# Two heads at a time on the array's halves, columns spread by transposes, and the modulation's products moved to TensorE

## The chip, the cores and the metric

The kernel runs on one core of one Trainium2 chip. The metric is the device time of one execution in microseconds. Times are shown as the median of several runs, with the lowest and the highest; a profile is of one execution, and its span is the time from its first to its last instruction.

## The reference

The program is a stack of four residual blocks on 256 positions of width 1024, in fp32. The first block has two layers; each layer mixes four branches (retention, short convolution, conformer convolution, windowed attention) on the sequence `x` and, in layer 0, on a context of 256 positions too. A second block of a recurrence, a gated linear attention and two feed-forward networks follows. The change touches the modulation of the first block, its attention, and the normalizations all over.

```python
def ada_modulation(cvec, w, b):
    m = jax.nn.silu(cvec) @ w + b                 # 1024 -> 3072
    return jnp.split(m, 3, axis=-1)

# per layer l of the first block, for c (sequence) and c_ctx (context)
shift_x, scale_x, gate_x = ada_modulation(c, w_mod[l], b_mod[l])
shift_c, scale_c, gate_c = ada_modulation(c_ctx, w_mod[l], b_mod[l])
hx = modulate(rmsnorm(x, norm_w[l]), shift_x[:, None], scale_x[:, None])
...
x = x + gate_x[:, None] * out_x

def windowed_gqa(q, k, v, k_ctx, v_ctx, sink):    # 8 heads of 64, 2 kv heads, window 128
    s_loc = jnp.einsum('bnqhgd,bnkhd->bnhgqk', qb, kw) * scale   # masked
    s_ctx = jnp.einsum('bnqhgd,bchd->bnhgqc', qb, k_ctx) * scale
    p = jax.nn.softmax(jnp.concatenate([s_loc, s_ctx, s_sink], axis=-1), axis=-1)
    o = (jnp.einsum('bnhgqk,bnkhd->bnqhgd', p_loc, vw)
         + jnp.einsum('bnhgqc,bchd->bnqhgd', p_ctx, v_ctx))
```

In layer 0 the context's own 256 queries attend to the context's keys as well.

## The kernel before

Activations lie transposed, channels on partitions and positions along the free dimension: tiles of 128 channels by 256 positions, or by 512 in layer 0 (sequence and context side by side). Every projection is a sum of three fp32r products: `load` fetches a weight chunk of 128x1024 (512 KB), ScalarE rounds it to `wh`, VectorE makes the rest `wl`, and `mm3` multiplies high by high, high by low and low by high. Chunks come in a fixed order (`mixer_chunks`); four are held at a time, and `drop` lets the next be fetched.

Beside this stream, work is queued. `hiq` holds generators (attention, convolutions, layer norm, retention), each `yield` with a cost; `loq` holds (cost, function) pairs for the rest. After each output tile `pump(us)` adds credit and runs the queues: `hiq` at full rate, `loq` at `ratio` times the rate (0.5 in layer 0 until the layer norm is done, then 1.4), from the eleventh pump of layer 0 on, with a credit of at most 4. A scheduler then orders each engine's instructions by this emission order and its own estimate of when each is ready; each engine works strictly through its list.

The modulation of layer 0's first two thirds (shift and scale) is made at the start by `products` and `columns`: eight matmuls whose stationary operand has 32 columns (two are used: the silu of `c` and of `c_ctx`), in four column strips of the array, then a copy to SBUF and two small matmuls with the selector `sel` that add the four strips and turn rows into columns. The rest (layer 0's gate and all of layer 1, 32 tiles of 128 columns) is queued on `loq` by `queue_mods`: `fetch_row` brings 128x1024 of the transposed weight, and `matvec` runs one VectorE pass per condition with an accumulator (line 487). Behind them in `loq` stand 96 such rows, with one pass each, for the modulation of the second block (`adaT`); `flush_lo` runs what is left at the end of a layer. The rows' pool has two buffers, and the SyncE queue that fetches rows fetches the weight chunks too.

`att_head` handles one head: scores for each block of 128 queries (64 contraction rows, on partitions 0 to 63 or 64 to 127 by the head's parity), a VectorE reduction that scales, masks and takes the maximum (lines 1077 and 1089), exponentials on ScalarE, a division on VectorE, transposes of the probabilities on TensorE (line 1110), and products with the values (64 stationary columns) into the head's half of a PSUM tile that two heads share (`outs`). `attention` runs the eight heads in a pipe of two.

`spread` makes a 128x128 tile whose rows all repeat one column: an fp32 product of the broadcast column with the identity. Normalizations use it, two to eight at a time.

PSUM has four banks for projections (`psm`) and four for all else (`psa`).

Of the kernel before, what the change touches and what calls it, by code (L numbers as in the profile page):

```python
# [18 lines left out]
P = 128  # L19
D = 1024  # L20
KT = 8
# [83 lines left out]
class Core:  # L105
# [324 lines left out]
    def spread(self, out, col):  # L430

        self.mmul(out, col.to_broadcast([P, P]), self.ident)
# [26 lines left out]
    def silu_load(self, name):  # L459
        t = self.adp.tile([P, 1024], F32, tag="sb", bufs=2, name="sb_" + name)  # L460
# [30 lines left out]
    def queue_mods(self, sc, sx):  # L491
        A, cst = self.A, self.cst
        self.done_mods = [0, 0, 0]
        self.gate = [cst.tile([P, 8, 2], F32, name=f"gate{l}") for l in range(2)]

        def one(l, t):
            m = self.mod[l]
            self.matvec([sc, sx], [m[:, t, 0:1], m[:, t, 1:2]])

        def fin(l):  # L500
            m = self.mod[l]
            lo = 16 if l == 0 else 0
            self.tt(m[:, lo:24, :], m[:, lo:24, :],
                    self.par("b_mod", l * 24 + lo, 24 - lo).unsqueeze(2).to_broadcast([P, 24 - lo, 2]), ALU.add)
            self.ts(self.gate[l], m[:, 16:24, :], 0.5, ALU.mult)
            if l == 1:
                self.stt(self.acol, m[:, 8:16, :], 1.0,
                         self.par("norm_w", 8, 8).unsqueeze(2).to_broadcast([P, KT, 2]), ALU.add, ALU.mult)
            self.done_mods[l] = 1
# [42 lines left out]
    def start(self):  # L552
# [26 lines left out]
        s32 = self.T(S).rearrange("p (k n) -> p k n", k=KT)  # L579
# [5 lines left out]
        def products(g):  # L585

            ps = self.psa()[:, :S]
            for kk in range(KT):
                c = slice((kk % 2) * S, (kk % 2 + 1) * S)
                o = 32 * (kk % 4)  # L590
                nc.tensor.matmul(out=ps[o:o + 32, :], lhsT=s32[:, kk, :], rhs=raws[g][kk // 2][:, c],
                                 start=kk < 4, stop=kk > 3, skip_group_check=True)
            rws[g] = self.rowp.tile([P, 512], F32, tag="row", name=self.nm("row"))[:, :S]
            self.act(rws[g], ps)
# [17 lines left out]
        sel = cst.tile([P, 2], F32, name="sel")  # L612
        nc.vector.tensor_reduce(out=sel, in_=self.ident.rearrange("p (u m) -> p m u", u=4)[:, 0:2, :], axis=AX.X, op=ALU.add)
        def columns(g):
            pm = self.psa()[:, 0:4]
            for t in range(2):
                self.mmul(pm[:, 2 * t:2 * t + 2], rws[g][:, t * P:(t + 1) * P], sel)
            k = 2 * (g // 2)
            p3 = pm.rearrange("p (t n) -> p t n", n=2)
# [104 lines left out]
    def prepare(self):  # L724
        cst = self.cst
        with self.behind():
# [7 lines left out]
            self.queue_mods(*[self.silu2_rows(self.silu_load(n)) for n in ("c", "c_ctx")])  # L734
# [131 lines left out]
    def mixer(self, l, hs, N, first, mod, norm):  # L866
# [193 lines left out]
        outs = {}  # L1060

        def att_head(h):
            t, u = divmod(h, 2)
            g = h // 4
            r = slice(64 * u, 64 * u + 64)
            sink = self.par("att_sink", l * 8 + h)
            nr = 2 * NS
            mx, sm, es = self.small(nr), self.small(nr), self.small(nr)
            ss = []
            for i in range(2):  # L1070
                ps = self.psa()
                lq = qs[t][r, i * P:(i + 1) * P]
                c0 = 0 if i == 0 else S
                self.mmul(ps[:, c0:c0 + S], lq, kd[g][r, 0:S])
                self.mmul(ps[:, S - c0:2 * S - c0], lq, kd[g][r, S:2 * S])
                s = self.T()
                nc.vector.tensor_tensor_reduce(out=s, in0=ps, in1=msk[i], scale=0.125, scalar=sink,
                                               op0=ALU.add, op1=ALU.max, accum_out=mx[:, i:i + 1])
                ss.append(s)
                yield 0.7  # L1080
            if NS == 2:
                ps = self.psa()
                s = self.T()
                for i in range(2):
                    c = slice(i * S, (i + 1) * S)
                    self.mmul(ps[:, c], qs[t][r, S + i * P:S + (i + 1) * P], kd[g][r, S:2 * S])
                for i in range(2):
                    c = slice(i * S, (i + 1) * S)
                    nc.vector.tensor_tensor_reduce(out=s[:, c], in0=ps[:, c], in1=msk[0][:, S:], scale=0.125,
                                                   scalar=sink, op0=ALU.add, op1=ALU.max,  # L1090
                                                   accum_out=mx[:, 2 + i:3 + i])
                    ss.append(s[:, c])
                yield 0.8
            self.ts(mx, mx, -1.0, ALU.mult)
            self.act(es, mx, AF.Exp, bias=sink)
            for i, s in enumerate(ss):
                self.act(s, s, AF.Exp, bias=mx[:, i:i + 1], accum_out=sm[:, i:i + 1])
            yield 0.1
            self.tt(sm, sm, es, ALU.add)
            nc.vector.reciprocal(out=sm, in_=sm)  # L1100
            for i, s in enumerate(ss):
                self.ts(s, s, sm[:, i:i + 1], ALU.mult)
            yield 0.2 + 0.6 * NS
            PT = []
            for i in range(1 + NS):
                pt, p = self.psa(), self.T()
                src = ss[i] if i < 2 else None
                for kk in range(4):
                    blk = ss[i][:, kk * P:(kk + 1) * P] if i < 2 else ss[2 + kk // 2][:, (kk % 2) * P:(kk % 2 + 1) * P]
                    nc.tensor.transpose(pt[:, kk * P:(kk + 1) * P], blk, self.ident)  # L1110
                self.act(p, pt)
                PT.append(p)
                yield 0.1
            if u == 0:
                outs[t] = self.psa()
            po = outs[t]
            for i in range(nr):
                toks = ((0, 1, 2, 3), (2, 3, 0, 1), (2, 3), (2, 3))[i]
                src = PT[i] if i < 2 else PT[2][:, (i - 2) * S:(i - 1) * S]
                for kk, tk in enumerate(toks):  # L1120
                    self.mmul(po[r, i * P:(i + 1) * P], vt[:, tk * P + g * 64:tk * P + g * 64 + 64],
                              src[:, kk * P:(kk + 1) * P], kk == 0, kk == len(toks) - 1)
                if i == 1:
                    yield 0.1
            if u == 1:
                self.act(qs[t], po[:, :N])
                if t == 3:
                    st["att"] = 1
# [692 lines left out]
def build(nc, tc, A):  # L1821
    with ExitStack() as ctx:
        k = Core(nc, tc, ctx, A)
        with ExitStack() as c1:
            k.adp = c1.enter_context(tc.tile_pool(name="adp", bufs=2, reuse_waits="tile"))
            k.setup()
            k.t2 = c1.enter_context(tc.tile_pool(name="t2", bufs=58, reuse_waits="tile"))
# [7 lines left out]
def pack(a):  # L1835
# [10 lines left out]
    wmT = wm.transpose(0, 2, 1).reshape(48, P, 1024)  # L1846
# [9 lines left out]
        "c": f("c").reshape(1, 1024), "c_ctx": f("c_ctx").reshape(1, 1024), "c_2": f("c_2").reshape(1, 1024),  # L1856
        "wmodN": wm[0][:, 0:2048].reshape(4, 2, P, 2, 4, 256)[:, :, :, ::-1].transpose(4, 3, 0, 2, 1, 5).reshape(8, 4, P, 512),
        "wmodT": wmT[16:48],
# [27 lines left out]
```

## Time and profile before

| | |
|---|---|
| median of 3 runs | 1828.62 us (1828.25 to 1831.88) |
| the profiled execution | 1827.48 us, of which its span is 1825.4 us |
| TensorE (PE) busy | 1772.5 us, 97% |
| VectorE (DVE) busy | 1395.3 us, 76% |
| ScalarE (ACT) busy | 892.6 us, 49% |
| read from HBM | 298.61 MB, 164 GB/s over the span |

A busy share is the time in which at least one instruction of the engine was at work, so overlapping matmuls count once. The duration of a matmul record reaches from its start to its modelled end; in a stream the records start closer together than they last. PE is the matmuls, PEld the loads of the stationary operand, POOL is GpSimd, SP is SyncE. `pm` are tiles in the projections' banks, `pa` tiles in the others, `wr` raw weight chunks, `ad` the modulation's rows, `t`, `r` and `s` working tiles, `junk` the unused product of a matrix-vector pass. PEclk is the granted TensorE clock as a share of 2.4 GHz.

### The profile page before, as it was taken

What the parts mean: (1) busy time and instruction counts of PE and PEld (TensorE: products, weight loads), DVE (VectorE), ACT (ScalarE), POOL (GpSimd) and SP (SyncE); (2) the same over time, 40 slices, a digit from 0 to 9 for tenths busy, and PEclk for the clock granted to TensorE, in tenths of its full rate; (3) what the DMA queues carried; (4) which work ended last, traced back from release to release, by engine and by line L of the source; (5) the groups of instructions that cost most, each with busy time, mean ns of one, the idle gap of its engine ahead of it and who ended that gap; (6) DMA issues with size and microseconds to landing.
All of it is one profiled execution on the core that took longest, in us unless ns stands there. A gap on an engine that the chain in (4) does not pass through costs nothing.

```text
span 1825.4 us, 29814 instructions
## 1 busy us (share of the span) xinstructions
PE 1772.5 (97%) x11604; PEld 1589.0 (87%) x11604; DVE 1395.3 (76%) x2564; ACT 892.6 (49%) x1517; POOL 9.4 (1%) x33
## 2 busy tenths in 40 slices
PE   8999999899999998999999999999999999999998
PEld 5788888688978777798999989988999999989998
DVE  4897689975687888899559666778888679788774
ACT  5424432422342223455453455677676656657663
POOL 0000000000000000000000000000000000000000
PEclk9999999999999999999999999999999999999999
DMA  8443234344557787744345335553455643345553
GB/s 335 136 138 105 71 104 159 130 162 163 176 187 263 266 267 264 249 147 132 116 131 171 109 115 175 187 183 104 152 195 179 180 139 105 116 132 193 185 172 117
DMA packets 94300, 301.59 MB, mean 165 GB/s; under 512 B 10048, under 2 KB 11840, under 8 KB 94160
## 3 DMA queue, kind: packets, MB, share of 16 engines
q1 hardware_dynamic: 90528, 292.11, 48.3%
q0 software_dynamic: 1152, 4.19, 0.6%
q10 hardware_dynamic: 2480, 3.39, 0.6%
q8 instruction: 91, 1.49, 0.3%
q14 instruction: 49, 0.40, 0.1%
HBM read 298.61 MB, written 1.05 MB: 164 GB/s over the span
## 4 chain that ended last, share of the span: by engine, by line
PE 79%; DVE 9%; DMA 6%; ACT 3%; issue 3%; SPq 0%; DVEq 0%; ACTq 0%
PE pm L189 60%; PE pa L189 17%; DMA ad<-adaT 5%; DVE junk L487 2%; DVE wl L169 2%; ACT t L166 2%; DVE t L186 1%; PE pa L1110 1%; DVE t L169 1%; ACT wh L166 1%; DMA t<-wmodN 1%; PE pa L539 1%; PE pa L1703 1%; PE pa L400 1%; DVE x L169 0%
## 5 line engine op out<-in xcount | busy, mean ns | idle before, releaser
L189 PE MATMUL pm<-r,wh 128*128 128x256 f32 (+2 forms) x5344 | 1217.3, 322 | 30.5 <-ACT r L166 18.1
L189 PEld LDWEIGHTS pm<-r,wh 128*128 128x128 f32 x5344 | 891.6, 191 | 124.3 <-ACT r L166 25.1
L189 PE MATMUL pm<-r,wl 128*128 128x256 f32 (+2 forms) x2672 | 848.1, 319 | 0.5 <-DVE wl L169 0.5
L166 ACT ACTIVATE wh<-wr 128x1024 fp32r<-128x1024 f32 (+1 forms) x408 | 426.1, 1049 | 558.1 <-PE pm L189 385.7
L169 DVE TENSOR_TENSOR wl<-wr,wh 128x1024 fp32r<-128x1024 f32 (+1 forms) x408 | 492.6, 1211 | 212.6 <-ACT wh L166 208.1
L189 PEld LDWEIGHTS pm<-r,wl 128*128 128x128 f32 x2672 | 510.1, 191 | 36.2 <-DVE wl L169 0.9
L487 DVE SCALAR_TENSOR_TENSOR junk<-ad,sb_c 128x1024 bf16<-128x1024 f32 x128 | 156.3, 1221 | 41.8 <-DMA ad<-adaT 40.2
L189 PE MATMUL pa<-r,wh 128*128 128x256 f32 (+1 forms) x864 | 170.7, 295 | 5.2 <-ACT r L166 4.6
L189 PEld LDWEIGHTS pa<-r,wh 128*128 128x128 f32 x864 | 139.7, 195 | 8.8 <-ACT r L166 5.0
L169 DVE TENSOR_TENSOR t<-t,t 128x256 f32<-128x256 f32 (+2 forms) x278 | 126.4, 470 | 15.6 <-ACT t L166 13.4
L186 DVE SCALAR_TENSOR_TENSOR t<-t,cfw,t 128x482 f32<-128x482 f32 (+29 forms) x240 | 130.5, 600 | 0.0
L189 PE MATMUL pa<-r,wl 128*128 128x256 f32 (+1 forms) x432 | 125.8, 295 | 0.0
L189 PE MATMUL pa<-t,t 128*64 128x128 f32 (+3 forms) x668 | 117.3, 337 | 0.2 <-DVE t L186 0.2
L166 ACT ACTIVATE r<-t 128x256 fp32r<-128x256 f32 (+1 forms) x116 | 53.5, 469 | 109.9 <-DVE t L169 76.6
L189 PEld LDWEIGHTS pa<-t,t 128*64 128x64 f32 (+2 forms) x668 | 90.1, 163 | 18.1 <-issue 5.7
L166 ACT ACTIVATE t<-pm 128x256 f32<-128x256 f32 (+1 forms) x180 | 82.3, 457 | 19.1 <-PE pm L189 19.1
L189 PEld LDWEIGHTS pa<-r,wl 128*128 128x128 f32 x432 | 84.4, 195 | 1.3
L166 ACT ACTIVATE t<-pa 128x512 f32<-128x512 f32 (+2 forms) x102 | 47.5, 509 | 66.0 <-PE pa L189 43.3
L189 PE MATMUL pm<-wh,r 128*128 128x256 f32 x384 | 71.9, 285 | 0.0
L186 DVE SCALAR_TENSOR_TENSOR t<-t,pm 128x256 f32<-128x256 f32 (+1 forms) x103 | 56.1, 545 | 6.6 <-PE pm L189 5.3
L189 PEld LDWEIGHTS pm<-wh,r 128*128 128x128 f32 x384 | 60.5, 191 | 0.5 <-issue 0.4
L169 DVE TENSOR_TENSOR r<-t,r 128x256 fp32r<-128x256 f32 (+1 forms) x108 | 51.0, 479 | 10.7 <-ACT r L166 10.7
(209 smaller groups left out, 1262.2 us busy)
## 6 DMA issues: line engine op xcount, KB each, us to landing
wr<-win SPq DMA_DIRECT2D x172, 512.0 KB, 3.4
ad<-adaT SPq DMA_DIRECT2D x96, 512.0 KB, 4.3
wr<-ffu SPq DMA_DIRECT2D x88, 512.0 KB, 3.3
ad<-wmodT SPq DMA_DIRECT2D x32, 512.0 KB, 3.3
wr<-wbr SPq DMA_DIRECT2D x32, 512.0 KB, 4.2
wr<-ffd SPq DMA_DIRECT2D x32, 512.0 KB, 3.6
wr<-gli SPq DMA_DIRECT2D x24, 512.0 KB, 3.3
t<-wmodN SPq DMA_DIRECT2D x32, 256.0 KB, 5.2
```

Of the source, the lines that this page charges most:

```text
L166: return self.nc.scalar.activation(out=out, in_=in_, func=func, **k)
L169: self.marks.append(self.nc.vector.tensor_tensor(out=out, in0=a, in1=b, op=op).ins)
L186: self.marks.append(self.nc.vector.scalar_tensor_tensor(out=out, in0=a, scalar=s, in1=b, op0=op0, op1=op1).ins)
L189: self.nc.tensor.matmul(out=out, lhsT=lhsT, rhs=rhs, start=start, stop=stop)
L400: self.nc.tensor.matmul(out=rows, lhsT=lhsT, rhs=t, start=(first and i == 0), stop=(last and i == len(tiles) - 1), skip_group_check=True)
L487: self.nc.vector.scalar_tensor_tensor(out=self.junk, in0=raw, scalar=0.5, in1=v, op0=ALU.mult, op1=ALU.mult, accum_out=o)
L539: self.nc.tensor.matmul(out=bank[:, nt * j + t:nt * j + t + 1], lhsT=q[:, t * P:(t + 1) * P], rhs=self.inv[inv], start=first and m == 0 an ...
L1110: nc.tensor.transpose(pt[:, kk * P:(kk + 1) * P], blk, self.ident)
L1703: nc.tensor.matmul(out=o, lhsT=cb[:, 7 - jj:7 - jj + P], rhs=b8(hd_(X, h))[:, :, jj:8], start=(jj == 0 and h % 2 == 0), stop=(jj == 7), sk ...
```

## The change

Three edits. `spread` becomes a transpose of the broadcast column. Attention goes by pairs of heads: the two heads of a tile issue their score matmuls alternately into two PSUM tiles, and their value products alternately into the two halves of one; the pairs run one after the other instead of a pipe of two heads. The rest of the first block's modulation is made like its beginning, by products with 32 stationary columns: 16 groups of 256 columns in two halves of four contraction tiles (queue cost 1.0 each), a copy, two selector matmuls and one addition (cost 0.5); the weight is packed anew for it (`wmodM`, 32 pieces of 512 KB), and the broadcast copies of `c` and `c_ctx` go. The rows' pool has three buffers instead of two, the broadcast vector one instead of two, and the first block's working pool 57 instead of 58.

```diff
     def spread(self, out, col):
-        self.mmul(out, col.to_broadcast([P, P]), self.ident)
+        self.nc.tensor.transpose(out, col.to_broadcast([P, P]), self.ident)
...
+    def column_products(self, ps, kks, w):
+        for kk in kks:
+            o = 32 * (kk % 4)
+            self.nc.tensor.matmul(out=ps[o:o + 32, :], lhsT=self.s32[:, kk, :], rhs=w(kk),
+                                  start=kk < 4, stop=kk > 3, skip_group_check=True)
+
+    def product_rows(self, ps):
+        rw = self.rowp.tile([P, 512], F32, tag="row", name=self.nm("row"))[:, :S]
+        self.act(rw, ps)
+        return rw
+
+    def product_columns(self, rw):
+        pm = self.psa()[:, 0:4]
+        for t in range(2):
+            self.mmul(pm[:, 2 * t:2 * t + 2], rw[:, t * P:(t + 1) * P], self.sel)
+        return pm.rearrange("p (t n) -> p t n", n=2)
...
-    def queue_mods(self, sc, sx):
+    def queue_mods(self):
...
-        def one(l, t):
-            m = self.mod[l]
-            self.matvec([sc, sx], [m[:, t, 0:1], m[:, t, 1:2]])
...
+        acc = {}
+        def half(g, j):
+            for _ in range(2 - len(self.raws)):
+                self.fetch_row()
+            raw = self.raws.popleft()
+            if j == 0:
+                acc[g] = self.psa()[:, :S]
+            self.column_products(acc[g], range(4 * j, 4 * j + 4), lambda kk: raw[:, (kk % 4) * S:(kk % 4 + 1) * S])
+            self.fetch_row()
+            if j == 1:
+                acc[g] = self.product_rows(acc[g])
+        def put(g):
+            l, t = (0, 16 + 2 * g) if g < 4 else (1, 2 * g - 8)
+            self.tt(self.mod[l][:, t:t + 2, :], self.product_columns(acc.pop(g)),
+                    self.par("b_mod", l * 24 + t, 2).unsqueeze(2).to_broadcast([P, 2, 2]), ALU.add)
...
-        for l in range(2):
-            for t in range(16 if l == 0 else 0, 24):
-                self.rows.append(A["wmodT"][t - 16 if l == 0 else 8 + t])
-                self.loq.append((2.3, lambda l=l, t=t: one(l, t)))
-            self.loq.append((0.3, lambda l=l: fin(l)))
+        for g in range(16):
+            for j in range(2):
+                self.rows.append(A["wmodM"][g, j])
+                self.loq.append((1.0, lambda g=g, j=j: half(g, j)))
+            self.loq.append((0.5, lambda g=g: put(g)))
...
-            self.queue_mods(*[self.silu2_rows(self.silu_load(n)) for n in ("c", "c_ctx")])
+            self.queue_mods()
...
-        def att_head(h):
...
+        def att_pair(t):
+            g, nr = t // 2, 2 * NS
+            rs = [slice(64 * u, 64 * u + 64) for u in range(2)]
...
+            for i in range(2):
+                ps = [self.psa(), self.psa()]
                 c0 = 0 if i == 0 else S
+                for o, j in ((c0, 0), (S - c0, S)):
+                    for u, r in enumerate(rs):
+                        self.mmul(ps[u][:, o:o + S], qs[t][r, i * P:(i + 1) * P], kd[g][r, j:j + S])
+                for u in range(2):
+                    s = self.T()
+                    nc.vector.tensor_tensor_reduce(out=s, in0=ps[u], in1=msk[i], scale=0.125, scalar=sink[u],
+                                                   op0=ALU.add, op1=ALU.max, accum_out=mx[u][:, i:i + 1])
+                    ss[u].append(s)
+                    yield 0.7
...
+            po = self.psa()
             for i in range(nr):
                 toks = ((0, 1, 2, 3), (2, 3, 0, 1), (2, 3), (2, 3))[i]
                 for kk, tk in enumerate(toks):
+                    for u, r in enumerate(rs):
+                        src = PT[u][i] if i < 2 else PT[u][2][:, (i - 2) * S:(i - 1) * S]
+                        self.mmul(po[r, i * P:(i + 1) * P], vt[:, tk * P + g * 64:tk * P + g * 64 + 64],
+                                  src[:, kk * P:(kk + 1) * P], kk == 0, kk == len(toks) - 1)
...
-            yield from self.pipe([att_head(h) for h in range(8)], 2)
+            for t in range(4):
+                yield from att_pair(t)
...
-            k.adp = c1.enter_context(tc.tile_pool(name="adp", bufs=2, reuse_waits="tile"))
+            k.adp = c1.enter_context(tc.tile_pool(name="adp", bufs=3, reuse_waits="tile"))
```

## Rows read from the trace of the kernel before

**Rows 1.** The page's busy times: us, share of the span, instructions.
```profile
PE 1772.5 (97%) x11604; PEld 1589.0 (87%) x11604; DVE 1395.3 (76%) x2564; ACT 892.6 (49%) x1517; POOL 9.4 (1%) x33
```
**Rows 2.** The chain that ended last, shares by engine.
```profile
PE 79%; DVE 9%; DMA 6%; ACT 3%; issue 3%; SPq 0%; DVEq 0%; ACTq 0%
```
**Rows 3.** Stretches: length, busy us (instructions) per engine, granted clock, DMA share, GB/s.
```profile
123.00:333.00 210.00, 209.34 (x1077) 171.15 (x1076) 173.98 (x333) 79.33 (x154) 0.00 (x0) 1.00 0.34 115
640.00:709.00 69.00, 65.33 (x279) 53.40 (x279) 57.10 (x85) 20.50 (x28) 0.00 (x0) 0.95 0.79 262
```
**Rows 4.** Groups by shape: count | busy us, mean ns | idle before, what ended it.
```profile
L166 ACT ACTIVATE wh<-wr 128x1024 fp32r<-128x1024 f32 x392 | 413.0, 1058 | 540.9 <-PE pm L189 369.4 <-issue 85.9 <-PE pa L189 45.5
L487 DVE SCALAR_TENSOR_TENSOR junk<-ad,sb_c 128x1024 bf16<-128x1024 f32 x128 | 156.3, 1221 | 41.8 <-DMA ad<-adaT 40.2 <-DMA ad<-wmodT 1.4
...
L189 PE MATMUL pa<-t,t 128*64 128x128 f32 x320 | 37.3, 276 | 0.0
...
L189 PE MATMUL pa<-t,t 64*128 64x256 f32 x160 | 33.3, 394 | 0.0
...
L1077 DVE CUSTOM_DVE_ANT_0 t<-pa,t,prm 128x512 f32<-128x512 f32 x32 | 23.6, 748 | 17.5 <-PE pa L189 17.0
...
L166 ACT ACTIVATE t<-pa 128x256 f32<-128x256 f32 x39 | 12.6, 382 | 16.0 <-PE pa L189 15.7
```
**Rows 5.** Timeline of TensorE: start, us to the last end, count; score products.
```profile
135.84 2.10 PE L189 MATMUL pa<-t,t 64*128 64x256 f32 x16
...
143.58 1.13 PE L189 MATMUL pa<-t,t 64*128 64x256 f32 x4
```
**Rows 6.** Two short stretches of TensorE alone, inside value products.
```profile
158.61:158.99 0.38, 0.38 (x9) 1.00 0.37 119
155.80:156.20 0.40, 0.40 (x5) 1.00 0.98 369
```
**Rows 7.** Timeline of TensorE: four spreads by products, four transposes.
```profile
348.47 1.05 PE L189 MATMUL pa<-ident,s 128*128 128x128 f32 x8
...
151.19 0.60 PE L1110 MATMUL pa<-ident,t 128*128 128x128 f32 x4
```
**Rows 8.** Timeline of TensorE at the start: products with 32 columns, the selector.
```profile
34.02 0.40 PE L189 MATMUL pm<-r,wl 128*128 128x512 f32 x1
34.35 1.07 PE L591 MATMUL pa<-t,t 128*32 128x256 f32 x16
35.35 0.73 PE L189 MATMUL pm<-r,wh 128*128 128x512 f32 x2
35.92 0.39 PE L189 MATMUL pm<-r,wl 128*128 128x512 f32 x1
36.15 0.62 PE L189 MATMUL pm<-r,wh 128*128 128x512 f32 x2
...
36.84 0.50 PE L189 MATMUL pa<-sel,row 128*128 128x2 f32 x4
37.20 0.49 PE L189 MATMUL pm<-r,wh 128*128 128x512 f32 x1
```
**Rows 9.** Stretches, line 487 on VectorE alone: length, busy us (instructions), clock, DMA.
```profile
640.00:709.00 69.00, 29.80 (x49) 0.95 0.79 262
709.00:767.00 58.00, 24.22 (x40) 0.94 0.78 266
```
**Rows 10.** Waits from 500 to 775 us: total, times, longest.
```profile
DVE junk L487 <- DMA ad<-adaT: 38.3, 36, 3.0
```
**Rows 11.** Timeline of TensorE at 714 us, with the idle time before it.
```profile
714.03 1.22 PE L189 MATMUL pm<-r,wh 128*128 128x512 f32 x2 [4.74 <-ACT r L166]
```
**Rows 12.** Three stretches, all engines, columns as in rows 3.
```profile
635.00:645.00 10.00, 2.75 (x7) 1.09 (x6) 9.27 (x14) 2.85 (x5) 0.00 (x0) 0.80 0.83 260
...
714.00:719.40 5.40, 5.37 (x13) 4.23 (x14) 4.68 (x7) 2.27 (x5) 0.00 (x0) 0.50 0.75 276
756.00:774.00 18.00, 13.73 (x112) 13.14 (x111) 14.75 (x29) 8.29 (x14) 0.00 (x0) 1.00 0.64 213
```

More of the change, by code (lines that the diff above doesn't have):

```diff
@@ L459, in silu_load @@
     def silu_load(self, name):
-        t = self.adp.tile([P, 1024], F32, tag="sb", bufs=2, name="sb_" + name)
+        t = self.adp.tile([P, 1024], F32, tag="sb", bufs=1, name="sb_" + name)
         with self.behind():
@@ L578, in start @@
         self.act(th, self.cc, AF.Tanh, scale=0.5)
-        s32 = self.T(S).rearrange("p (k n) -> p k n", k=KT)
+        self.s32 = s32 = self.adp.tile([P, KT, 32], F32, name="s32", tag="s32", bufs=1)
         nc.gpsimd.memset(s32, 0.0)
@@ L587, in products @@
             ps = self.psa()[:, :S]
[L588 to L594, printed above, removed]
+            self.column_products(ps, range(KT), lambda kk: raws[g][kk // 2][:, (kk % 2) * S:(kk % 2 + 1) * S])
+            rws[g] = self.product_rows(ps)
         sq = []
@@ L611, in start @@
         self.ts(bs1, self.par("b_mod", 8, 8), 1.0, ALU.add)
-        sel = cst.tile([P, 2], F32, name="sel")
+        self.sel = sel = cst.tile([P, 2], F32, name="sel")
         nc.vector.tensor_reduce(out=sel, in_=self.ident.rearrange("p (u m) -> p m u", u=4)[:, 0:2, :], axis=AX.X, op=ALU.add)
         def columns(g):
-            pm = self.psa()[:, 0:4]
-            for t in range(2):
-                self.mmul(pm[:, 2 * t:2 * t + 2], rws[g][:, t * P:(t + 1) * P], sel)
             k = 2 * (g // 2)
-            p3 = pm.rearrange("p (t n) -> p t n", n=2)
+            p3 = self.product_columns(rws[g])
             bc = lambda v: v.unsqueeze(2).to_broadcast([P, 2, 2])
@@ L1058, in att_prep @@
             yield 0.1
-        outs = {}
-        def att_head(h):
[L1063 to L1069, printed above, removed]
+        def att_pair(t):
+            g, nr = t // 2, 2 * NS
+            rs = [slice(64 * u, 64 * u + 64) for u in range(2)]
+            sink = [self.par("att_sink", l * 8 + 2 * t + u) for u in range(2)]
+            mx, sm, es = [[self.small(nr) for _ in range(2)] for _ in range(3)]
+            ss = [[], []]
@@ L1070, in att_head @@
             for i in range(2):
-                ps = self.psa()
-                lq = qs[t][r, i * P:(i + 1) * P]
+                ps = [self.psa(), self.psa()]
                 c0 = 0 if i == 0 else S
[L1074 to L1078, printed above, removed]
@@ L1079, in att_head @@
-                ss.append(s)
-                yield 0.7
+                for o, j in ((c0, 0), (S - c0, S)):
[7 more added lines that the diff above has]
+                    yield 0.7
@@ L1081, in att_head @@
             if NS == 2:
-                ps = self.psa()
-                s = self.T()
+                ps = [self.psa(), self.psa()]
                 for i in range(2):
                     c = slice(i * S, (i + 1) * S)
[L1086 to L1104, printed above, removed]
@@ L1105, in att_head @@
-            for i in range(1 + NS):
[L1106 to L1115, printed above, removed]
@@ L1116, in att_head @@
-            po = outs[t]
+                    for u, r in enumerate(rs):
+                        self.mmul(ps[u][:, c], qs[t][r, S + i * P:S + (i + 1) * P], kd[g][r, S:2 * S])
+                for u in range(2):
+                    s = self.T()
+                    for i in range(2):
+                        c = slice(i * S, (i + 1) * S)
+                        nc.vector.tensor_tensor_reduce(out=s[:, c], in0=ps[u][:, c], in1=msk[0][:, S:], scale=0.125,
+                                                       scalar=sink[u], op0=ALU.add, op1=ALU.max,
+                                                       accum_out=mx[u][:, 2 + i:3 + i])
+                        ss[u].append(s[:, c])
+                    yield 0.8
@@ new lines, in att_pair @@
+            for u in range(2):
+                self.ts(mx[u], mx[u], -1.0, ALU.mult)
+                self.act(es[u], mx[u], AF.Exp, bias=sink[u])
+                for i, s in enumerate(ss[u]):
+                    self.act(s, s, AF.Exp, bias=mx[u][:, i:i + 1], accum_out=sm[u][:, i:i + 1])
+                yield 0.1
+            for u in range(2):
+                self.tt(sm[u], sm[u], es[u], ALU.add)
+                nc.vector.reciprocal(out=sm[u], in_=sm[u])
+                for i, s in enumerate(ss[u]):
+                    self.ts(s, s, sm[u][:, i:i + 1], ALU.mult)
+                yield 0.2 + 0.6 * NS
@@ new lines, in att_pair @@
+            PT = [[], []]
+            for i in range(1 + NS):
+                for u in range(2):
+                    pt, p = self.psa(), self.T()
+                    for kk in range(4):
+                        s = ss[u][i][:, kk * P:(kk + 1) * P] if i < 2 else ss[u][2 + kk // 2][:, (kk % 2) * P:(kk % 2 + 1) * P]
+                        nc.tensor.transpose(pt[:, kk * P:(kk + 1) * P], s, self.ident)
+                    self.act(p, pt)
+                    PT[u].append(p)
+                    yield 0.1
@@ L1117, in att_head @@
+            po = self.psa()
             for i in range(nr):
                 toks = ((0, 1, 2, 3), (2, 3, 0, 1), (2, 3), (2, 3))[i]
-                src = PT[i] if i < 2 else PT[2][:, (i - 2) * S:(i - 1) * S]
                 for kk, tk in enumerate(toks):
-                    self.mmul(po[r, i * P:(i + 1) * P], vt[:, tk * P + g * 64:tk * P + g * 64 + 64],
-                              src[:, kk * P:(kk + 1) * P], kk == 0, kk == len(toks) - 1)
+                    for u, r in enumerate(rs):
+                        src = PT[u][i] if i < 2 else PT[u][2][:, (i - 2) * S:(i - 1) * S]
+                        self.mmul(po[r, i * P:(i + 1) * P], vt[:, tk * P + g * 64:tk * P + g * 64 + 64],
+                                  src[:, kk * P:(kk + 1) * P], kk == 0, kk == len(toks) - 1)
@@ L1123, in att_head @@
                 if i == 1:
[L1124 to L1128, printed above, removed]
+                    yield 0.2
+            self.act(qs[t], po[:, :N])
+            if t == 3:
+                st["att"] = 1
             yield 0.1
@@ L1824, in build @@
         with ExitStack() as c1:
-            k.adp = c1.enter_context(tc.tile_pool(name="adp", bufs=2, reuse_waits="tile"))
+            k.adp = c1.enter_context(tc.tile_pool(name="adp", bufs=3, reuse_waits="tile"))
             k.setup()
-            k.t2 = c1.enter_context(tc.tile_pool(name="t2", bufs=58, reuse_waits="tile"))
+            k.t2 = c1.enter_context(tc.tile_pool(name="t2", bufs=57, reuse_waits="tile"))
             fin = k.first_block()
@@ L1845, in pack @@
     wm = f("w_mod")
-    wmT = wm.transpose(0, 2, 1).reshape(48, P, 1024)
+    wmod = wm.transpose(0, 2, 1).reshape(6144, 1024)[2048:]
     up = kn(f("ffn_w_up_2"))
@@ L1855, in pack @@
         "xT": np.concatenate([f("x")[0].T, f("ctx")[0].T], 1).reshape(8, P, 512),
-        "c": f("c").reshape(1, 1024), "c_ctx": f("c_ctx").reshape(1, 1024), "c_2": f("c_2").reshape(1, 1024),
+        "c_2": f("c_2").reshape(1, 1024),
         "wmodN": wm[0][:, 0:2048].reshape(4, 2, P, 2, 4, 256)[:, :, :, ::-1].transpose(4, 3, 0, 2, 1, 5).reshape(8, 4, P, 512),
-        "wmodT": wmT[16:48],
+        "wmodM": wmod.reshape(16, 256, 2, 4, P).transpose(0, 2, 4, 3, 1).reshape(16, 2, P, 1024),
         "adaT": f("ada_w_2").transpose(0, 2, 1).reshape(96, P, 1024),
```

15 lines of the change are left out of this document (6 added, 9 removed).

## The prediction

> **What bounds the kernel now.** I read the busy shares first: TensorE is busy for 97% of a span of 1825.4 us [rows 1], and the chain that ended last runs on TensorE for 79% of the span and on VectorE for 9% [rows 2]. The reader should see from this that the kernel is a stream of matmuls that is seldom starved, so that a microsecond of TensorE work saved or added counts almost whole. Next I cut the first block into stretches. From 123 to 333 us (the second part of layer 0's mixer, where the modulation's matrix-vector products begin) TensorE is idle for 0.7 of 210 us while VectorE is busy for 174: VectorE sets nothing there. From 640 to 709 us (the last gated projections of layer 0) TensorE is idle for 3.7 of 69 us and the granted clock falls to a mean of 0.95 [rows 3]. The time that VectorE costs is concentrated there and right behind, and it has to be priced by its events, not by its total.
>
> **Attention in pairs.** By the grouped instructions, the score products of single heads (64 contraction rows, 256 columns) are 160 records that together occupy 33.3 us, and the products with the values (64 stationary columns) are 320 records that occupy 37.3 us; an fp32 product leaves two records [rows 4]. What a pair is worth can be read in the trace of before, where the order happens to put two heads beside each other. Four score records of one head take 1.13 us, 0.28 each with the ends; the sixteen records at 135.84 us, of two heads, take 2.10 us, 0.131 each, so two halves of the array did work at once [rows 5]. At that rate 160 records take 21.0 us; I take 22, since in a group that stands alone the first and the last record have no partner. That is 11 us saved. The values' products overlap in a few places only: in 0.38 us at 158.61 nine records are in flight, against five in 0.40 us at 155.80 [rows 6]. Half of 37.3 is 18.7; I take 20, so 17 us saved. Together 28 us; the bounds are 0 (the halves don't overlap when issued this way) and 35 (both halve entirely, 70.6 / 2). The transposes, reductions, exponentials and divisions stay as many as they were.
>
> VectorE has to empty the scores' banks: 0.748 us for each head and 512 columns [rows 4], against some 0.53 us of TensorE for the same head at the paired rate (four records at 0.131 us). The Trainium skill, TensorEngine Tiling (Array Packing), section Performance Considerations (PSUM Bottleneck), says that tiling speeds up TensorE but not the emptying of PSUM, which may become the limit. By that rule the scores' 11 us would not arrive and the sum would end near 1826 us; by the row of this stretch VectorE has room (174 of 210 us busy, and the matrix-vector passes leave it) and I keep the 11. The same thing as a mechanism is a rival below.
>
> **Columns spread by transposes.** The code spreads 66 columns: 14 for normalizations in the first block (4 at its start, 6 in the layer norms, 4 ahead of layer 1), 24 in the retentions, 4 at the start of the second block, 16 at the four block ends, 8 in the gated attention. A spread by a product leaves two records, a transpose one: eight records for four columns took 1.05 us at 348.47, four transposes took 0.60 us at 151.19, so 0.45 us for four columns [rows 7] and 66 / 4 x 0.45 = 7.4 us. All of it lies on TensorE; in the block ends it lies in the chain as well. I take 7; the bounds are 5 (where TensorE waits for the column anyway) and 7.4.
>
> **The rest of the modulation.** Removed: 64 passes over 1024 columns on VectorE, 32 for each condition, at 1.221 us and 0.08 us for reading the accumulator, 83 us [rows 4]; two broadcast loads, two tanh and two passes of 1024 columns before them. Between 123 and 333 us this buys nothing directly, as TensorE never waits there [rows 3]. Added on TensorE: 32 half groups of four products with 32 stationary columns, 8 records each, and 16 times two small products with the selector. The trace has both, from the start: sixteen records of the first kind took 1.00 us from 34.35 until the next projection matmul, the pair of matmuls behind them 0.73 us instead of 0.62, and the matmul ahead of them lasted until they began, 0.33 us instead of 0.23: 1.21 in all [rows 8]. Half as many go in two steps fewer; a step of 256 columns is some 0.22 us (2.10 us for eight such steps, less the ends [rows 5]), so 0.78. So 32 x 0.78 = 25.0 us, or 16 x 1.21 = 19.4 where two halves stand together. Four selector records took 0.36 us until the next matmul, 0.40 with its slower start: 6.4 us for 16 [rows 8]. Sum 26 to 31; I take 29.
>
> The rows' copy out of PSUM is 0.382 us of ScalarE, 16 times [rows 4]; ScalarE is busy for 79 of 210 us there [rows 3], so 6 us hide in its idle time. The additions on VectorE are tens of elements. The 32 transfers stay 32 of 512 KB, on the same queue; they come in about 60% of the time, at a DMA share of 0.34 now [rows 3]. What is new is who waits: TensorE itself stands behind a row that has not landed, and behind ScalarE's copy between a group's products and its selector products. The order can put projection matmuls there; for what it misses I take 0.2 us a group, 3 us, with 0 and 23 as bounds (the latter below).
>
> **What VectorE gives back.** The rest queue spends a budget that grows with TensorE's tiles. It charged 32 x 2.3 + 2 x 0.3 = 74.2 for the modulation and will charge 16 x 2.5 = 40. The 34.2 left over pay for 34.2 / 1.15 = 30 of the 96 matrix-vector rows of the second block's modulation, which begin behind it; these 30 go out before 503 us instead of at the end. In before, VectorE's instructions on that line (two a row) say 24 rows in 640 to 709 us and 20 after 709 [rows 9]. Thirty fewer leave 14 of the 44 behind 640 us, which at that rate are done some 40 us on, before 709. That also takes away waits: VectorE stood for 38.3 us in 36 places for these transfers between 500 and 775 us [rows 10], with every VectorE instruction behind it in line; the third buffer for rows shortens the others.
>
> The price: at 709 us TensorE waits 4.74 us for the last split of the merged tile, which stands behind two such rows on VectorE [rows 11], and then works at half clock (0.50 of 2.4 GHz, the 1.2 level) until 719.4, 5.4 us in which 2.7 are lost; from 756 to 774 us it is idle for 4.3 us, with rows still on VectorE, and from 635 to 645 us for 7.3 us [rows 12]. I take 7.4 us for the first event whole (4.7 and 2.7), 3 of the second (part of it is the layer's own normalization) and 1 of the third, which the rows still reach: 11 us. Bounds: 0, if something else is late next, and 19 with all three events whole.
>
> **The sum.** -28 - 7 + 29 + 3 - 11 = -14 us on the profiled execution's 1827.48 us, 1813.5; the median of the runs shown is 1.1 us above that execution, so 1815.
>
> **Rivals.**
> Slower, by one mechanism: in every group TensorE stands for ScalarE's copy. If a weight's split (1.058 us) is ahead of the copy (0.382) in ScalarE's line [rows 4], a group costs 1.44 us, 16 of them 23 us instead of 3: 1835 us. For it: engines work strictly in order, and both steps of a group may be issued at once. Against: in 123 to 333 us TensorE lost only 0.7 us although layer norm and softmax have the same round trips [rows 3]. It decides from (14 + 3) / 16 = 1.1 us a group. Chance 0.11.
> VectorE paces the pairs: two banks are taken at once, a third may hold an unfinished group of the modulation, and the next pair waits for 0.748 us per head; the scores' 11 us stay away: 1826 us. For it the duration [rows 4], against it VectorE's freed time. Chance 0.12.
> The rows of the second block's modulation end too late, or another piece of VectorE's work is late at 709 us: no 11 us there, 1826 us. For it: the stretch 640 to 709 is close to my end of the rows. Against: without them VectorE has less than half of its work there. Chance 0.13.
> The pairing does nothing, because a product's two records must follow each other on one half before the other half starts: 28 us are missing, 1843 us. Against it the sixteen records [rows 5]. Chance 0.04.
>
> **How the numbers follow.** My forecast has 0.60, at 1815 us, with its own range of 1802 to 1826 (products 26 to 31, waits up to 6, VectorE's part 4 to 19, attention 22 to 33). The 1826 of the two middle rivals lies within; the range for 8 in 10 reaches from 1800 to 1832 and leaves out the two slower cases (0.15) and a little below. About 0.2%, 3.7 us, is what a measurement of this kernel can tell from no change: faster is below 1825, slower above 1832.3. Faster: nearly all of 0.60 and somewhat under half of the two middle rivals' 0.25, 0.70. Slower: 0.15 and a little of their upper side, 0.16. Same: 0.14.
>
> **What would show it.** Right: score records that start in twos, 0.11 us apart on the mean, and both groups' busy time near 20 us; one record for each spread column; 256 records with 32 columns, in runs that cost about 0.8 us; the last matrix-vector row before 709 us, no wait of TensorE there, and no half clock behind it. Wrong: idle time of TensorE whose end is ScalarE's copy of a product row, a landing of the modulation's new array, or a reduction of the scores; wrong too if the gap at 709 us stays with the rows gone.

## The result and the profile after

The changed kernel takes 1802.74 us (median of 4 runs, 1801.68 to 1804.99) against 1830.25 us of the kernel before in the same job: ratio 0.9851, 95% interval 0.9834 to 0.9868, so 27 us (24 to 30) less. The forecast was 14 us less, 1815 us in a range of 1800 to 1832: the direction and the range hold, the size is half.

The page of the changed kernel, its span, its busy times and the chain by engine (columns as in [rows 1] and [rows 2]):

```profile
span 1801.1 us, 30219 instructions
PE 1758.3 (98%) x11858; PEld 1569.0 (87%) x11858; DVE 1323.4 (73%) x2448; ACT 894.4 (50%) x1531; POOL 9.5 (1%) x33
PE 84%; DVE 7%; ACT 4%; DMA 3%; issue 3%; DVEq 0%; SPq 0%; ACTq 0%
```

TensorE's busy time fell by 14 us, the span by 24: ten of them were idle time. The chain that ended last now runs on TensorE for 84% of the span instead of 79%. The groups by shape, changed kernel:

```profile
L189 PE MATMUL pa<-t,t 64*128 64x256 f32 x160 | 23.6, 397 | 0.4 <-DVE s L1098 0.4
L1098 DVE CUSTOM_DVE_ANT_0 t<-pa,t,prm 128x512 f32<-128x512 f32 x32 | 22.9, 746 | 18.1 <-PE pa L189 18.1
L477 PE MATMUL pa<-ad,s 128*32 128x256 f32 x256 | 20.4, 389 | 1.0 <-DVE s L1098 1.0
L189 PE MATMUL pa<-t,t 128*64 128x128 f32 x320 | 19.8, 276 | 0.3 <-ACT t L166 0.3
...
L189 PE MATMUL pa<-sel,row 128*128 128x2 f32 x96 | 12.5, 236 | 0.0
```

Scores occupy 23.6 us instead of 33.3, values 19.8 instead of 37.3 [rows 4]: 27 us where the sum had 28. The new products occupy 20.4 us. A score's reduction still lasts 0.746 us. VectorE stood for 18.1 us in all waiting for scores before such a reduction; TensorE stood for 1.4 us waiting for reductions (0.4 before scores, 1.0 before new products). A half group stands in the timeline of TensorE like this:

```profile
297.69 0.39 PE L189 MATMUL pm<-r,wl 128*128 128x512 f32 x1
298.01 0.64 PE L477 MATMUL pa<-ad,s 128*32 128x256 f32 x8
298.58 0.73 PE L189 MATMUL pm<-r,wh 128*128 128x512 f32 x2
```

From 298.01 to 298.58 it is 0.57 us; the matmul ahead lasts 0.32 until it begins instead of 0.23, and the pair behind 0.73 instead of 0.62: 0.77 in all, where the sum had 0.78. The stretches, changed kernel (columns as in [rows 3] and [rows 12]):

```profile
123.00:333.00 210.00, 208.46 (x1314) 159.98 (x1313) 129.77 (x268) 81.34 (x167) 0.00 (x0) 1.00 0.41 138
354.00:363.00 9.00, 9.00 (x43) 7.48 (x42) 7.68 (x12) 4.72 (x7) 0.00 (x0) 1.00 0.45 160
...
648.00:651.00 3.00, 3.00 (x9) 2.38 (x9) 2.65 (x9) 0.00 (x0) 0.00 (x0) 0.54 0.69 283
709.00:714.00 5.00, 5.00 (x24) 4.14 (x23) 2.06 (x4) 1.84 (x6) 0.00 (x0) 1.00 0.28 105
```

VectorE has 44 us less to do between 123 and 333 us. At 709 us TensorE works without a pause. Between 123 us and the passage to layer 1 one gap of more than 1 us is left, at 642.9 us, with a stretch near half clock (0.54) behind it:

```profile
646.67 1.09 PE L189 MATMUL pm<-r,wh 128*128 128x512 f32 x3 [3.75 <-ACT r L166]
```

And one stretch above was not on the list of the prediction: from 354 to 363 us TensorE is busy throughout. The same stretch of before, and the one behind it:

```profile
354.00:363.00 9.00, 4.05 (x11) 2.01 (x10) 9.00 (x18) 4.01 (x6) 0.00 (x0) 0.70 0.38 116
363.00:368.00 5.00, 5.00 (x12) 3.23 (x12) 5.00 (x9) 1.65 (x3) 0.00 (x0) 0.51 0.01 5
```

TensorE idles there for 4.95 us while VectorE is busy for all 9, and then works at half clock for 5.

To place gains along the way, one can count the matmul records with 512 columns (line 189): all kernels here have the same 2698, nearly all of them layer 0's projections, so the time of the n-th is progress through the same work. Worked out from the traces, us between the n-th and the m-th:

```
kernel                       400-1000  1000-1200  2000-2200  2200-2400  2400-2600
before                          190.3       58.0       55.5       52.9      109.2
after                           205.1       48.6       51.4       45.3      106.6
spreads alone                   190.3       57.1       55.7       53.6      109.2
pairs alone                     177.4       56.5       57.0       54.1      109.8
modulation alone                219.1       49.6       55.6       45.3      106.6
modulation alone, late rows     203.8       53.6       57.3       46.6      106.6
modulation alone, two buffers   219.1       49.7       55.3       45.3      106.6
three buffers alone             190.3       58.0       54.1       49.7      106.6
short passes alone              190.1       48.6       55.6       53.8      109.1
after, two buffers              205.1       48.6       56.1       45.3      106.6
after, ratio 0.7                205.1       48.6       45.3       45.3      106.4
after, ratio 0.7, joined        199.4       48.6       45.3       45.3      106.2
```

The columns are the attention with most of the modulation, the stall at 354 us, the one at 640, the one at 709, and the passage to layer 1 at 756. Where TensorE works without a pause at full clock, 200 of these records take 45.3 us, so the third column has 10 us of loss in before and the fourth 8. Each row is one execution. Behind the last column lies work that most of these edits leave alone, and there before, the modulation alone (all three forms) and the short passes took 994 to 999 us: a difference of a few us between two spans is not a reading.

### The profile page after: what moved, and what is told of

The parts are those of the page before. It is cut to its first block, busy times and chain, and to the rows that moved or that the text cites. A ratio compares the mean times of both kernels' runs of the same rounds, so it can differ in the third digit from the quotient of the medians.

```text
span 1801.1 us, 30219 instructions
## 1 busy us (share of the span) xinstructions
PE 1758.3 (98%) x11858; PEld 1569.0 (87%) x11858; DVE 1323.4 (73%) x2448; ACT 894.4 (50%) x1531; POOL 9.5 (1%) x33
## 4 chain that ended last, share of the span: by engine, by line
PE 84%; DVE 7%; ACT 4%; DMA 3%; issue 3%; DVEq 0%; SPq 0%; ACTq 0%
PE pm L189 64%; PE pa L189 15%; DVE wl L169 2%; ACT t L166 2%; DMA ad<-adaT 2%; PE pa L477 1%; ACT wh L166 1%; DVE t L186 1%; DVE t L169 1%; DVE junk L507 1%; PE pa L1135 1%; PE pa L569 1%; PE pa L1727 1%; PE pa L400 1%; DVE x L169 0%
## 5 line engine op out<-in xcount | busy, mean ns | idle before, releaser
L507 DVE SCALAR_TENSOR_TENSOR junk<-ad,sb_c 128x1024 bf16<-128x1024 f32 x96 | 117.2, 1221 | 20.1 <-DMA ad<-adaT 19.3
L189 PE MATMUL pa<-t,t 128*64 128x128 f32 (+3 forms) x668 | 89.7, 337 | 0.8 <-DVE s L1098 0.4
L189 PEld LDWEIGHTS pa<-t,t 128*64 128x64 f32 (+2 forms) x668 | 67.3, 163 | 16.2 <-issue 5.4
L186 DVE SCALAR_TENSOR_TENSOR t<-t,pm 128x256 f32<-128x256 f32 (+1 forms) x103 | 56.1, 545 | 11.8 <-PE pm L189 9.7
L169 DVE TENSOR_TENSOR r<-t,r 128x256 fp32r<-128x256 f32 (+1 forms) x108 | 51.0, 479 | 10.5 <-ACT r L166 10.4
```

Source lines behind the costliest of these rows:

```text
L169: self.marks.append(self.nc.vector.tensor_tensor(out=out, in0=a, in1=b, op=op).ins)
L186: self.marks.append(self.nc.vector.scalar_tensor_tensor(out=out, in0=a, scalar=s, in1=b, op0=op0, op1=op1).ins)
L189: self.nc.tensor.matmul(out=out, lhsT=lhsT, rhs=rhs, start=start, stop=stop)
L507: self.nc.vector.scalar_tensor_tensor(out=self.junk, in0=raw, scalar=0.5, in1=v, op0=ALU.mult, op1=ALU.mult, accum_out=o)
```

## The experiments

**One part of the three at a time.** Theory: the prediction's terms, -7 for the spreads, -28 for the pairs, and +29 + 3 - 11 for the modulation.

`e1_spread`, only the spread:

```diff
-        self.mmul(out, col.to_broadcast([P, P]), self.ident)
+        self.nc.tensor.transpose(out, col.to_broadcast([P, P]), self.ident)
```

> Only the spreads become transposes. By the sum of the prediction: 7 us less than before (5 to 7.4), since every record saved lies on TensorE. Rival: half of the spreads stand where TensorE waits for the column anyway, so 3 to 4 us. Nothing moves in the rows of the second block's modulation; the idle time of TensorE at 354 to 362, 635 to 645 and 709 us stays.

Ratio 0.9968 (0.9957 to 0.9978), 6 us less (4 to 8). TensorE has 66 instructions fewer than before (11604 in [rows 1]), one for each column as counted:

```profile
PE 1769.2 (97%) x11538; PEld 1583.9 (87%) x11538; DVE 1395.1 (76%) x2564; ACT 892.7 (49%) x1517; POOL 9.6 (1%) x33
```

At two block ends a part of the time comes back as waiting. TensorE at the second spread of one of them, before and with the spread alone:

```profile
1478.39 0.71 PE L189 MATMUL pa<-ident,s 128*128 128x128 f32 x4 [0.27 <-DVE s L1441]
```

```profile
1476.59 0.43 PE L432 MATMUL pa<-ident,s 128*128 128x128 f32 x2 [0.55 <-DVE s L1441]
```

Two records fewer ahead of it, and TensorE stands there 0.28 us longer (0.55 against 0.27): there VectorE's column sets the end. The two places cost 0.6 us together; whether the rest of the difference from 7 is real the interval doesn't tell.

`e2_pairs`, only the attention: `att_head` and its pipe replaced by `att_pair`.

> Only the attention goes by pairs; the modulation stays on VectorE. By the sum: 24 to 28 us less than before, as the records of scores and values start two by two (in the changed kernel they are 43 us from start to start instead of 69). Rival (VectorE paces the pairs): with the passes of the modulation still on VectorE, the reductions free the banks late, TensorE waits inside the pairs, and only some 15 us come. The idle times of TensorE after 354 us stay, so what is saved in layer 0 may in part be waited away behind.

Ratio 0.9854 (0.9839 to 0.9869), 27 us less. The rival is out: with all passes still on VectorE the scores occupy

```profile
L189 PE MATMUL pa<-t,t 64*128 64x256 f32 x160 | 21.8, 397 | 0.0
```

and the gain is 12.9 us in the first column of the table and 13.4 in layer 1, from its first score to its last product with values. The stalls of layer 0 stay (6.2 us at 697 us).

`e3_mods`, only the modulation (`queue_mods`, its three helpers, buffers).

> Only the modulation moves to TensorE (with the third row buffer and the 57 working tiles). By my terms: +29 on TensorE, -11 from VectorE, +3 of waits: 21 us slower than before. By the trace of the changed kernel, in which the half clock at 357 and 712 us is gone and the fixed number of projection matmuls gains some 20 us between 320 and 720 us: 5 to 8 us slower. If VectorE's part were the pairs' doing and not the modulation's, 25 us slower or more.

Ratio 1.0046 (1.0029 to 1.0063), 8 us slower (5 to 12). By the table it loses 28.8 us where the products lie and gets back 8.4, 7.6 and 2.6 us. So the three parts give -6, -27 and +8: -24 together before rounding, the whole change -27, within the intervals.

**Why VectorE's part is larger.** Theory: the second block's rows start early and end before 709 us. Rival: the passes that are gone, or the third buffer.

`e4_mods_late`: as `e3_mods`, the rows start as late as before.

```diff
-                self.loq.append((1.0, lambda g=g, j=j: half(g, j)))
+                self.loq.append((2.05, lambda g=g, j=j: half(g, j)))
```

> As the run with the modulation alone, but each half group is charged 2.05 instead of 1.0, so that a group costs what two of the old tiles did and the second block's rows start as late as before. Theory (the rows end earlier): the gap at 709 us and its half clock are back, 44 rows stand behind 640 us, and the time is 10 to 20 us above the run with the modulation alone. Rival (it is the 64 passes taken off VectorE before 430 us, or the third buffer, that count): no more than 5 us above it, and no gap at 709 us.

Ratio 1.0062 (1.0041 to 1.0083), 3 us above `e3_mods` (5 by the medians), no gap behind the gated projections: against the theory. The rows began at 475 us, and the last one ended at 737, just ahead of the 2400th record at 739. The edit also stretches the products themselves, which end at 467 us instead of 345; that is why the first column is smaller here and the second larger.

`e5_three_bufs`: the kernel before with a third buffer.

```diff
-            k.adp = c1.enter_context(tc.tile_pool(name="adp", bufs=2, reuse_waits="tile"))
+            k.adp = c1.enter_context(tc.tile_pool(name="adp", bufs=3, reuse_waits="tile"))
-            k.t2 = c1.enter_context(tc.tile_pool(name="t2", bufs=58, reuse_waits="tile"))
+            k.t2 = c1.enter_context(tc.tile_pool(name="t2", bufs=56, reuse_waits="tile"))
```

> The kernel before with three buffers for the modulation's rows instead of two (and 56 working tiles instead of 58, for the room); nothing else. Theory now (it is the third buffer that spares VectorE its waits for rows between 500 and 775 us): those 38 us of waits shrink to less than half, the gap at 709 us and the half clock behind it go, and the time is 8 to 10 us less than before; the stall at 354 to 362 us stays. Rival (the buffer is idle weight, and the passes on VectorE count): no change beyond 2 us, gap at 709 us as before.

Ratio 0.9936 (0.9911 to 0.9961), 12 us less (7 to 16). VectorE's waits for rows between 500 and 775 us, 38.3 us of before [rows 10], are

```profile
DVE junk L487 <- DMA ad<-adaT: 15.9, 21, 1.5
```

the rows end at 714 us instead of 766, and of the gap of 4.74 us [rows 11] this is left, without a fall of the clock behind it:

```profile
711.50 0.97 PE L189 MATMUL pm<-r,wh 128*128 128x512 f32 x3 [1.55 <-ACT r L166]
```

With smaller pieces ahead of it, TensorE still idles for 3.3 us in the fourth column, which falls from 52.9 to 49.7 and not to 45.3. The stall at 354 us stays. The table's columns show 7 us of the 12. One buffer, a line of the change that looks like housekeeping, is worth 12 us when it is made alone, where the whole change is worth 27.

`e6_mods_two_bufs`: `e3_mods` with `bufs=2`.

> The run with the modulation alone, with two row buffers instead of three. Theory (third buffer): the waits for rows and the gap behind the last gated projections come back, 7 to 12 us slower than the run with the modulation alone, though the rows still begin early. Rival (the early rows, as in the prediction): within 3 us of that run, with no such gap, since the rows end early all the same.

Ratio 1.0056 (1.0039 to 1.0073), 2 us above `e3_mods`, within the noise. VectorE waits more for rows again, 26.4 us where `e3_mods` has 12.0,

```profile
DVE junk L507 <- DMA ad<-adaT: 26.4, 22, 2.7
```

but they end at 701 us, 36 us ahead of the 2400th record, and the fourth column of the table is the same 45.3. So, with the 64 passes gone, each of the two does it alone: early rows with two buffers, or late rows with three. The theory of the prediction is sufficient, and not necessary.

`e8_after_two_bufs`: the changed kernel with `bufs=2`.

> The changed kernel with two row buffers instead of three. If early rows and the third buffer each remove the gap at 709 us by themselves, the buffer is worth little here: within 4 us of the changed kernel, rows ending near 680 us, waits of VectorE for rows near 45 us again, and no gap of over 4 us behind 650 us other than the one the changed kernel has. Rival: the products' rows need the third buffer as well; TensorE then waits for landings of the new array and the time is 10 us or more above.

Ratio 0.9880 (0.9863 to 0.9897), 5 us above the changed kernel, a little more than expected, with intervals that touch. TensorE never waits for a landing of the new array. What grows is the stall at 640 us, 56.1 us against 51.4 in the third column (two buffers, then three; all engines):

```profile
635.00:655.00 20.00, 12.80 (x42) 8.92 (x42) 17.83 (x28) 5.25 (x8) 0.00 (x0) 0.74 0.81 270
```

```profile
635.00:655.00 20.00, 16.09 (x63) 12.37 (x63) 18.12 (x35) 7.58 (x11) 0.00 (x0) 0.91 0.71 244
```

`e7_short_passes`: the kernel before, the 64 passes over 2 columns; the sums, and so the output, are not the reference's.

```diff
-            self.matvec([sc, sx], [m[:, t, 0:1], m[:, t, 1:2]])
+            self.matvec([sc, sx], [m[:, t, 0:1], m[:, t, 1:2]], 2)
```

> The kernel before, whose 64 passes over the first block's modulation rows take 2 of 1024 columns, so that these sums are not the reference's; transfers, order and everything else stay. Theory (the stall at 354 to 362 us and its half clock are those passes' doing): that stall goes, 7 to 9 us less than before, and the gap at 709 us stays. Rival (the stall belongs to the layer norm): less than 2 us of change.

Ratio 0.9952 (0.9937 to 0.9967), 9 us less (6 to 12). The stall is gone, the one at 700 us is not:

```profile
354.00:363.00 9.00, 9.00 (x41) 7.33 (x40) 7.24 (x22) 4.06 (x6) 0.00 (x0) 1.00 0.52 177
```

```profile
704.93 1.22 PE L189 MATMUL pm<-r,wh 128*128 128x512 f32 x2 [5.30 <-ACT r L166]
```

This is the missing piece: the passes themselves, not the rows behind them, made TensorE wait at 354 us. The run also settles the other half of the rival: with the passes short, but late rows and two buffers, the gap at 709 us stays, so the passes are not what removes it. Few of the passes lie inside the stall: in before they take 1.3 of VectorE's 9 us from 354 to 363, and 8.6 us from 320 to 354. The rest of those 9 us is VectorE's other work, which comes late.

**A better version.** `v1_slower_rows`: the changed kernel, the rows spread thinner.

```diff
-        self.ratio = (1.4, 1.0)[l]
+        self.ratio = (0.7, 1.0)[l]
```

> The changed kernel with the second block's rows spread thinner: the rest queue's ratio after the layer norm is 0.7 instead of 1.4. The changed kernel still loses 3.7 us of idle time at 643 us and some 1.7 us of half clock behind it, where VectorE has four passes for each output tile. If VectorE's lag is what the passes' density makes, that gap shrinks under 1 us and the time is 4 to 6 us below the changed kernel's, at 1797 to 1799 us. Rival: the gap belongs to the retention's end and stays; no change, or slower by a few us because rows reach into the output projections.

Ratio 0.9806 (0.9778 to 0.9834), 1795.75 us, 7 us below the changed kernel by the medians and a little more than expected, with intervals that touch. TensorE has no idle time left between 640 and 709 us, at full clock:

```profile
640.00:709.00 69.00, 69.00 (x306) 57.13 (x306) 55.84 (x89) 22.94 (x33) 0.00 (x0) 1.00 0.68 232
```

The gap belonged to the rows' density: 6.1 us in the table's third column against the changed kernel, 10.2 against before.

`v2_joined`: the same, with the halves of a group issued together.

```diff
-                self.loq.append((1.0, lambda g=g, j=j: half(g, j)))
+            self.loq.append((2.0, lambda g=g: (half(g, 0), half(g, 1))))
```

> The changed kernel with the ratio of 0.7, and the two halves of a group issued together (one entry of cost 2.0). Where two halves stand together they cost 1.09 us in the changed kernel's trace, alone 0.66 each and a slower matmul behind: 0.23 to 0.34 us a group, 16 groups, fewer since some stand together already. So 2 to 4 us below the run with the ratio alone, 1792 to 1794 us. Rival: two rows are used at once with three buffers, so TensorE waits for the next row's landing, and the gain is lost.

Ratio 0.9772 (0.9758 to 0.9787), 1788.67 us, 7 us below `v1_slower_rows` by the medians and by the spans (1786.3 against 1793.1), more than expected, though the intervals of the two ratios overlap. Two rows of it:

```profile
L189 PE MATMUL pa<-t,t 64*128 64x256 f32 x160 | 21.3, 396 | 0.0
L477 PE MATMUL pa<-ad,s 128*32 128x256 f32 x256 | 17.1, 385 | 1.0 <-DVE s L1098 1.0
```

The products occupy 3.3 us less than in the changed kernel, as expected, and the scores 2.3 us less, which was not. In the changed kernel single half groups had come between score records. One group of sixteen there (first three lines) runs in two pieces with products between them, and its last four records stand alone; with joined halves (last line) it runs in one piece:

```profile
135.81 1.99 PE L189 MATMUL pa<-t,t 64*128 64x256 f32 x12
137.73 0.62 PE L477 MATMUL pa<-ad,s 128*32 128x256 f32 x2
138.78 1.13 PE L189 MATMUL pa<-t,t 64*128 64x256 f32 x4 [0.43 <-DVE s L1098]
```

```profile
136.33 2.00 PE L189 MATMUL pa<-t,t 64*128 64x256 f32 x16
```

A second group of sixteen, at 188.57 us, has no products between, and yet half of its records start singly: 3.04 us until the next matmul instead of 1.93. What made its partners come late no run here shows; a bank that an unfinished half group holds would be one reason. The two rows' 5.6 us are about the 5.7 by which the table's first column falls.

## Why the prediction was right, and where it was too small

**Attention**: right. 28 us forecast, 27 measured alone. The halves overlap as the sixteen records [rows 5] promised, in the values' products as well, for which only a sliver was there to read [rows 6]. The rival in which VectorE paces the pairs did not come at its price: TensorE waits 1.4 us in all for the reductions. The rule of the Trainium skill, TensorEngine Tiling (Array Packing), section Performance Considerations, that the emptying of PSUM may become the limit, doesn't bind here. A piece of the rival may be the scores' 23.6 us, against 21.8 with the pairs alone and 21.3 with joined halves.

**Spreads**: 7 forecast, 6 measured (4 to 8). The lower bound's reason, waiting for the column at block ends, is seen in the rows, for 0.6 us.

**The modulation's products**: right. 29 and 3 of waits were forecast, 32; with the modulation alone the table's first column has 28.8, and the work ahead of it, where the first products lie, 1.4: 30. Idle time of TensorE from 123 to 333 us is 1.5 us in the changed kernel against 0.7. The rival of ScalarE's copy has no row: TensorE has no idle time before the selector products.

**What VectorE gives back**: the term that was mis-sized, 11 us with bounds of 0 and 19, against some 18.5 for the modulation alone (8.4, 7.6, 2.6) and 24 in the whole change (9.4, 4.1, 7.6, 2.6). Of its events, the one at 709 us and its follower were priced at 10.4 and gave 10. The stretch at 640 us was priced at 1, as rows would still reach it, and gave 4 in the changed kernel, 10 when the rows are spread; 14 rows were to be left behind 640 us, and 4 were. The step that failed is the sentence that taking 64 passes off VectorE "buys nothing directly": it was judged by the stretch from 123 to 333 us, but the last of the passes began at 423 us, and the stall at 354 us, idle time and half clock, was theirs; run alone, their removal is worth 9 us. It was there to see in the trace of before. The total still lies in the range because the other terms came out within 2 us of their forecasts and the range reached 15 us below the forecast.

**The mechanism at 709 us** holds in part: rows that begin early do remove the gap, and so does the third buffer where the passes are gone, which the prediction had only shortening waits. How much of the gap in the changed kernel is due to which has no answer, as each is enough.

Whether the 3 us by which the whole exceeds its parts are real stays open; the intervals don't tell. If they are, the table's third column is a place for them: no part alone gains there, and the whole gains 4.1.

## What to carry to other kernels

Where a strict in-order engine is 75% busy and the bound engine 97%, look for the windows in which the bound engine idles and the helper is at 100%. Work of the helper that comes in or just ahead of such a window counts, and so does the fall of the clock behind it: in before, the idle 4.95 and 4.74 us at 354 and 709 us were followed by 2.5 and 2.7 us lost at half clock. The same work elsewhere cost nothing that the table shows: with short passes the first column, where most of the passes lie, is the same (190.1 against 190.3). Spread low-priority work thin enough that the helper can follow; halving the rate at which rows were issued was worth about as much as the spreads. Half-array products pay when partners follow each other; here, keeping other shapes out of their groups and issuing small groups together was worth 6 to 7 us.

## What was not expected of the hardware

Products on different array halves or column strips overlap although each fp32 product leaves two records. Sixteen records of four strips cost 1.00 us [rows 8], 0.06 each, where four of one head cost 0.28 each [rows 5]. In the trace the sixteen start in fours, 0.007 us apart, with about 0.22 us from four to four. The four records of one head start 0.22 us apart or more, so four that start together are of four products: the first record of a product doesn't stand behind the second one of the product ahead. In which order the records stand in the engine's program the trace doesn't say. No alternation by hand at the level of records was needed: two heads alternating by product were enough to halve the values' time.
